# A streaming gradient kernel: the first store of every three tiles is issued after the second tile instead of the first

## The chip, the core and the metric

The kernel runs on one core of a Trainium2 chip. The metric is the device time of one execution in microseconds (us). The core's engines that do anything here are VectorE (DVE in the profile), GpSimd (POOL) and SyncE (SP), which only issues DMAs. All transfers between device memory and the on-chip memory go through the core's 16 DMA engines.

## What is computed

The input `x` is an 8192 x 8192 array of float32, and the output is its gradient along the rows:

```python
def reference(x):
    return np.gradient(x, axis=1)
```

Inside a row, an output element is half the difference of its two neighbours, `(x[j+1] - x[j-1]) / 2`. The first and the last element of a row are the plain differences `x[1] - x[0]` and `x[m-1] - x[m-2]`. The kernel reads 268 MB and writes 268 MB.

## The kernel before

The 8192 rows are cut into 32 tiles (`nsets`) of 256 rows; each of the 128 partitions holds two whole rows (`R = 2`), 16384 numbers or 64 KB, so a tile is 8 MiB. There are three buffers, `slots` (`NB = 3`), and a tile `i` uses slot `i % 3`. A slot is 64 numbers wider than the tile: the input is loaded at an offset of `SH = 64`, and the result is written in place at offset 0.

For each tile, in this order:

- `load(i)` (L60) brings the tile into its slot. It waits until the store of tile `i - 3`, which used the slot before, has landed.
- On POOL, `tensor_sub` (L70) takes the four plain differences of a partition's two rows and keeps them in the small buffer `ends`. It starts when the load has landed.
- On DVE, one custom instruction (L81) forms the halved differences of all 16382 inner elements of a partition. It follows the POOL instruction, since it overwrites the input.
- A copy (L92) puts the four numbers from `ends` into the result. The engine for it, `placer`, is POOL for tiles with `i % 5` of 1 or 3 (up to tile 29) and for tile 30, and DVE for the others.
- A store (L94) sends the tile out. It waits for the copy.

The last two tiles, 30 and 31, are done in two halves (one row of each partition at a time), each with its own copy and store of 4 MiB.

All loads and stores are issued by SP and go through one DMA queue, in program order: three loads, then, group by group, three stores and the three loads of the next group. The order is written out by hand (`tc.manual_schedule()`), and `chain` keeps only the waits that are needed. SP issues in order, so a store that waits holds up what stands behind it on SP. I call three tiles that share a turn of the slots a group: tiles 0 to 2, 3 to 5, and so on, ten full groups, then tiles 30 and 31.

Of the kernel before, what the change touches and what calls it, by code (L numbers as in the profile page):

```python
# [1 line left out]

# [4 lines left out]


@with_exitstack
def kernel(  # L10
    ctx: ExitStack,
    tc: tile.TileContext,
    x: bass.AP,
    out: bass.AP,
):

    nc = tc.nc
    P = nc.NUM_PARTITIONS
    n, m = x.shape
    R = 2
    NB = 3  # L30
    SH = 64
    W = R * m
    nsets = n // (P * R)
    f32 = x.dtype

    x_sets = x.rearrange("(s p t) m -> s p (t m)", p=P, t=R)
    out_sets = out.rearrange("(s p t) m -> s p (t m)", p=P, t=R)

    pool = ctx.enter_context(tc.tile_pool(name="pool", bufs=1))
    slots = [pool.tile([P, SH + W], f32, name=f"slot{k}", tag=f"slot{k}") for k in range(NB)]  # L40
    ends = pool.tile([P, nsets, R, 2], f32, name="ends", tag="ends")
    loads, stores = [], [None] * nsets
    in_front = {}

    def chain(i, ins, *needed):

        group, engine = f"slot{i % NB}", ins.ins.engine
        keep = [o.ins for o in needed]  # L50
        if in_front.get(engine, (None,))[0] == group:
            keep.append(in_front[engine][1])
        tc.declare_no_dep(ins.ins, group=group, keep=keep, reason="implied by the needed step")
        tc.add_to_no_dep_group(group, ins.ins)
        in_front[engine] = group, ins.ins
        return ins

    def load(i):
        b = slots[i % NB]
        ins = nc.sync.dma_start(out=b[:, SH : SH + W], in_=x_sets[i])  # L60
        loads.append(chain(i, ins, *([stores[i - NB]] if i >= NB else [])))

    with tc.manual_schedule():
        for i in range(NB):
            load(i)
        for i in range(nsets):
            b = slots[i % NB]
            xin = b[:, SH : SH + W].rearrange("p (t m) -> p t m", m=m)

            ins = nc.gpsimd.tensor_sub(  # L70
                out=ends[:, i, :, :],
                in0=xin[:, :, 1 : m : m - 2],
                in1=xin[:, :, 0 : m - 1 : m - 2],
            )
            at = [chain(i, ins, loads[i])]
            last = i >= nsets - 2
            nr = 1 if last else R
            for r in range(0, R, nr):
                c0, c1 = r * m + 1, (r + nr) * m - 1

                ins = nc.vector._custom_dve(  # L81
                    dve_ops.TENSOR_TENSOR_REDUCE_SUB_MAX,
                    out=b[:, c0:c1],
                    in0=b[:, SH + c0 + 1 : SH + c1 + 1],
                    in1=b[:, SH + c0 - 1 : SH + c1 - 1],
                    s0=0.0,
                    s1=0.5,
                )
                halved = chain(i, ins, *at)
                res = b[:, r * m : (r + nr) * m].rearrange("p (t m) -> p t m", m=m)  # L90
                placer = nc.gpsimd if i % 5 in (1, 3) and not last or i == nsets - 2 else nc.vector
                ins = placer.tensor_copy(out=res[:, :, 0 : m : m - 1], in_=ends[:, i, r : r + nr, :])  # L92
                placed = chain(i, ins, halved)
                ins = nc.sync.dma_start(  # L94
                    out=out_sets[i, :, r * m : (r + nr) * m], in_=b[:, r * m : (r + nr) * m]
                )
                stores[i] = chain(i, ins, placed)
                at = [halved]
            if i % NB == NB - 1:
                for k in range(i + 1, min(i + 1 + NB, nsets)):  # L100
                    load(k)


# [1 line left out]
_INS = ['x']  # L105
_OUTS = [((8192, 8192), 'float32')]


# [23 lines left out]
```

## Time and profile before

| what | value |
|---|---|
| time, median of 3 runs | 1247.57 us (1247.11 to 1249.06) |
| span of the profiled execution | 1245.5 us |
| DMA queue, share of 16 engines' span | 99.7%, 536.88 MB, 431 GB/s |
| DVE busy | 554.8 us, 45% |
| POOL busy | 17.7 us, 1% |
| a DVE instruction of a whole tile (L81) | 17.22 us, 30 times |
| a copy of the ends (L92), on DVE / on POOL | 0.17 / 0.19 us |

The span runs from the first to the last instruction of one profiled execution; the time of a run is some 2 us longer than it. The profile's timeline lists instructions with start, duration, engine, line, operation and tiles, and in brackets the idle time ahead of an instruction and what ended it. SPq is SyncE's queue; its rows merge several DMA issues into one ("x3"), so that the start is that of the first issue and the duration reaches to the last. A POOL row of L70 starts when a load has landed.

### The profile page before, as it was taken

How to read it: one execution, taken by the hardware profiler on the slowest of the kernel's cores; microseconds unless marked ns; L12 is line 12 of the kernel's file. 1: busy time of each engine (PE TensorE's matmuls, PEld its weight loads, DVE VectorE, ACT ScalarE, POOL GpSimd, SP SyncE). 2: the span in 40 equal slices, each digit the busy share in tenths (PEclk: the TensorE clock that was granted, in tenths of full speed). 3: DMA queues.
4: the chain of work that ended last, by engine and by line, in shares of the span. 5: the costliest groups of instructions: out<-in, count | busy, mean ns of one | idle time of the engine just before them, and what ended most of it. 6: DMA issues, size and time to landing. Idle time of an engine off the chain costs nothing.

```text
span 1245.5 us, 244 instructions
## 1 busy us (share of the span) xinstructions
DVE 554.8 (45%) x54; POOL 17.7 (1%) x50
## 2 busy tenths in 40 slices
DVE  2850583079009702850582079009603840591083
POOL 0000000000000000000000000000000000000020
DMA  9999999999999999999999999999999999999999
GB/s 404 438 436 434 413 436 438 438 438 436 434 427 434 425 438 438 436 438 438 427 425 434 431 438 438 438 436 429 427 431 431 438 436 436 436 429 434 434 396 404
DMA packets 9505, 536.88 MB, mean 431 GB/s; under 512 B 1056, under 2 KB 1056, under 8 KB 1056
## 3 DMA queue, kind: packets, MB, share of 16 engines
q1 hardware_dynamic: 9504, 536.88, 99.7%
q14 instruction: 1, 0.01, 0.0%
HBM read 268.44 MB, written 268.44 MB: 431 GB/s over the span
## 4 chain that ended last, share of the span: by engine, by line
another core or an unknown queue 74%; DVE 19%; DMA 3%; POOL 1%; issue 0%; SPq 0%; POOLq 0%
DVE slot L81 19%; DMA slot<-in_x_dram 3%; POOL slot L92 1%; POOL ends L70 0%; SPq L60 0%; DVE slot L92 0%; POOLq L127 0%
## 5 line engine op out<-in xcount | busy, mean ns | idle before, releaser
L81 DVE CUSTOM_DVE_ANT_0 slot<-slot 128x16382 f32<-128x16382 f32 (+1 forms) x34 | 551.5, 16219 | 668.4 <-POOL ends L70 668.3
L70 POOL TENSOR_TENSOR ends<-slot 128x4 f32<-128x4 f32 x32 | 6.3, 198 | 971.5 <-DMA slot<-in_x_dram 971.5
L92 POOL COPY slot<-ends 128x4 f32<-128x4 f32 (+1 forms) x14 | 11.2, 798 | 216.7 <-DVE slot L81 216.6
L92 DVE COPY slot<-ends 128x4 f32<-128x4 f32 (+1 forms) x20 | 3.4, 171 | 0.7
L116 POOL MEMSET const-float32-0.0<- 128x1 f32 x1 | 0.1, 99 | 0.2 <-issue 0.2
L116 POOL MEMSET const-bfloat16-1.0<- 128x1 bf16 x1 | 0.1, 102 | 0.0
L116 POOL MEMSET const-uint8-127<- 128x1 uint8 x1 | 0.1, 102 | 0.0
L116 POOL MEMSET const-float32-1.0<- 128x1 f32 x1 | 0.1, 98 | 0.0
## 6 DMA issues: line engine op xcount, KB each, us to landing
out_dram<-slot SPq DMA_DIRECT2D x4, 4096.0 KB, 20.2
slot<-in_x_dram SPq DMA_DIRECT2D x32, 58.0
out_dram<-slot SPq DMA_DIRECT2D x30, 40.4
```

Of the source, the lines that this page charges most:

```text
L70: ins = nc.gpsimd.tensor_sub(out=ends[:, i, :, :], in0=xin[:, :, 1 : m : m - 2], in1=xin[:, :, 0 : m - 1 : m - 2],)
L81: ins = nc.vector._custom_dve(dve_ops.TENSOR_TENSOR_REDUCE_SUB_MAX, out=b[:, c0:c1], in0=b[:, SH + c0 + 1 : SH + c1 + 1], in1=b[:, SH + c0 ...
L92: ins = placer.tensor_copy(out=res[:, :, 0 : m : m - 1], in_=ends[:, i, r : r + nr, :])
L116: nc = _bacc.Bacc("TRN2", target_bir_lowering=False, num_devices=1)
```

## The change

Stores move into a helper. For full groups, the store of the first tile is no longer issued when the first tile's copy is done, but with the second tile's: it waits for the first tile's copy and, by an added dependency, for the second tile's copy too. The second and third stores wait for their own copies as before, and the order on the queue and the transfers are the same. The rule for the engine of the copy changes as well: POOL copies the first tile of each group (`i % 3 == 0`, which takes in tile 30), DVE the other two. Tiles 30 and 31 keep their halves and their own stores.

```diff
+    def store(i, placed, cols=slice(0, W)):
+        ins = nc.sync.dma_start(out=out_sets[i, :, cols], in_=slots[i % NB][:, cols])
+        stores[i] = chain(i, ins, placed)
+        return ins
...
-                placer = nc.gpsimd if i % 5 in (1, 3) and not last or i == nsets - 2 else nc.vector
+                placer = nc.gpsimd if i % NB == 0 else nc.vector
                 ins = placer.tensor_copy(out=res[:, :, 0 : m : m - 1], in_=ends[:, i, r : r + nr, :])
                 placed = chain(i, ins, halved)
-                ins = nc.sync.dma_start(
-                    out=out_sets[i, :, r * m : (r + nr) * m], in_=b[:, r * m : (r + nr) * m]
-                )
-                stores[i] = chain(i, ins, placed)
                 at = [halved]
+                if last:
+                    store(i, placed, slice(r * m, (r + nr) * m))
+            if i % NB == 1 and not last:
+                opener = store(i - 1, first)
+                tc.add_manual_dep(
+                    opener.ins,
+                    placed.ins.name,
+                    mybir.DependencyInfo(mybir.DependencyClass.Sync, mybir.DependencyReason.DATA),
+                    reason="the first store of a group goes behind the second tile's difference",
+                )
+            first = placed
+            if i % NB and not last:
+                store(i, placed)
```

More of the change, by code (lines that the diff above doesn't have):

```diff
@@ L4 @@
 import concourse.tile as tile
-from concourse import bass_utils, dve_ops
+from concourse import bass_utils, dve_ops, mybir
 from concourse._compat import with_exitstack
@@ L90 @@
                 res = b[:, r * m : (r + nr) * m].rearrange("p (t m) -> p t m", m=m)
-                placer = nc.gpsimd if i % 5 in (1, 3) and not last or i == nsets - 2 else nc.vector
+                placer = nc.gpsimd if i % NB == 0 else nc.vector
                 ins = placer.tensor_copy(out=res[:, :, 0 : m : m - 1], in_=ends[:, i, r : r + nr, :])
                 placed = chain(i, ins, halved)
-                ins = nc.sync.dma_start(
-                    out=out_sets[i, :, r * m : (r + nr) * m], in_=b[:, r * m : (r + nr) * m]
-                )
-                stores[i] = chain(i, ins, placed)
-                at = [halved]
+                at = [halved]
+                if last:
[7 more added lines that the diff above has]
+                    reason="the first store of a group goes behind the second tile's difference",
+                )
+            first = placed
+            if i % NB and not last:
+                store(i, placed)
             if i % NB == NB - 1:
```

## The prediction

> **What bounds the kernel now.** I read the page first, then the timeline of one group of three tiles, then the end of the run. The page says that the DMA queue is the limit:
>
> ```profile
> span 1245.5 us, 244 instructions
> DVE 554.8 (45%) x54; POOL 17.7 (1%) x50
> q1 hardware_dynamic: 9504, 536.88, 99.7%
> ```
>
> The one hardware queue keeps the 16 DMA engines occupied for 99.7% of the span, while VectorE (DVE) works 45% of it. So no compute instruction matters by itself. What can matter is the few microseconds in which a DMA engine moves nothing, or moves slower than its pace.
>
> The timeline of tiles 3, 4 and 5 shows where those are. Columns: start, duration, engine, line, operation, tiles. The row of POOL L70 starts as soon as a load has landed, so I use it as the landing clock.
>
> ```profile
> 157.40 0.19 POOL L92 COPY slot<-ends 128x4 f32<-128x4 f32 x1 [17.32 <-DVE slot L81]
> 157.62 39.11 SPq L94 DMA_DIRECT2D out_dram<-slot  x3
> 159.24 0.20 POOL L70 TENSOR_TENSOR ends<-slot 128x4 f32<-128x4 f32 x1 [1.65 <-DMA slot<-in_x_dram]
> 159.47 17.22 DVE L81 CUSTOM_DVE_ANT_0 slot<-slot 128x16382 f32<-128x16382 f32 x1 [2.13 <-POOL ends L70]
> 176.72 0.17 DVE L92 COPY slot<-ends 128x4 f32<-128x4 f32 x1
> 178.71 0.20 POOL L70 TENSOR_TENSOR ends<-slot 128x4 f32<-128x4 f32 x1 [19.27 <-DMA slot<-in_x_dram]
> ```
>
> Load 4 has landed at 159.24, load 5 at 178.71. The store of tile 3 is issued at 157.62, so it sits in the queue behind load 5 for 21 us before it can move.
>
> Now the pace. Load 0 has landed at 22.62 and the last load, 31, at 1205.91; 61 transfers of 8 MiB lie between. Taking the landing rows of all second and third loads of a group, third minus second is 20.52 in the first group (62.46 - 41.94), and then 19.47, 19.58, 19.64, 19.94, 20.19, 19.56, 19.54, 19.33, 19.43. The five transfers from a third load to the next second load take 96.59 to 96.79 us (for example 275.42 - 178.71 = 96.71), which is 19.34 each. So the third load, and it alone, is stretched: by 1.18 us in the first group and by 0.13, 0.24, 0.30, 0.60, 0.85, 0.22, 0.20, -0.01 and 0.09 in the other nine, which add up to 2.62. Together 3.80 us. Check: 22.62 + 61 x 19.34 + 3.80 = 1206.2, and the row says 1205.91. All the time that this change can win back is in this 3.80 us.
>
> What is special about a third load? It is the only one that has a store queued behind it. The trace has a control for that, the last load:
>
> ```profile
> 1186.58 0.20 POOL L70 TENSOR_TENSOR ends<-slot 128x4 f32<-128x4 f32 x1 [77.07 <-DMA slot<-in_x_dram]
> 1195.56 8.91 POOL L92 COPY slot<-ends 128x2 f32<-128x2 f32 x2 [8.79 <-DVE slot L81]
> 1204.29 19.89 SPq L94 DMA_DIRECT2D out_dram<-slot  x4
> 1205.91 0.20 POOL L70 TENSOR_TENSOR ends<-slot 128x4 f32<-128x4 f32 x1 [1.44 <-DMA slot<-in_x_dram]
> ```
>
> Load 31 is also followed by a store, but that store is issued only at 1204.29, because the POOL copy that it waits for ran beside DVE and took 8.7 us. Load 31 took 1205.91 - 1186.58 = 19.33: no stretch. That is the order of events that the change makes everywhere.
>
> **What a late store costs.** Queued late, a store may find engines that have run dry. A table of short stretches prices the start; its last two columns count a packet where it begins, so a stretch with a rate is one in which packets start.
>
> ```profile
> 0.74:1.70 0.96, 0.00 (x0) 0.00 (x0) 1.00 0.00 0
> 1.70:2.40 0.70, 0.00 (x0) 0.00 (x0) 1.00 4.28 1498
> 1204.29:1205.10 0.81, 0.00 (x0) 0.18 (x1) 1.00 0.00 0
> 1205.10:1205.35 0.25, 0.00 (x0) 0.00 (x0) 1.00 4.63 1966
> 1205.35:1205.50 0.15, 0.00 (x0) 0.00 (x0) 1.00 0.51 218
> ```
>
> At the end of the run, 15 engines (1966 GB/s x 0.25 us = 15 packets of 32 KB) begin the store 0.8 to 1.06 us after its issue. The trace's rows of single packets put them at 0.85 to 0.99. The sixteenth begins at 1205.48, the moment it is done with load 31; that is 0.43 before the landing row. At the start of the run the same step takes longer: issue at 0.74, packets from 1.75 to 2.38, so 1.0 to 1.64.
>
> **The change, part by part.**
>
> *The first store of a group waits for the second tile's copy, ten times.* In the group shown, the new issue is at 176.72 + 0.17 + 0.03 = 176.92 instead of 157.62. By the end-of-run row its packets can begin at 177.77 to 177.91. Load 5 without the stretch has landed at 159.24 + 19.34 = 178.58, and its slowest engine is done 0.43 earlier, at 178.15. So the slowest engine, which sets the pace, has 0.24 us to spare; the faster ones wait up to half a microsecond, which costs nothing because they were ahead. Cost of the wait by this row: 0. By the start-up row: 176.92 + 1.64 = 178.56, that is 0.41 us late, and the first load had a slow first packet too (22.62 - 0.74 - 1.64 - 19.34 - 0.43 = 0.47). So 0.88 per hand-over, 8.8 us in ten. I take the end-of-run row, because it is this very hand-over, a store behind a load on running engines.
>
> [...]
>
> *The stretch goes.* In groups two to ten that is up to -2.62. Something may be left, since the store now arrives about 0.24 us before the slowest engine is done. I leave +0.2 for all nine. In the first group the 1.18 is four times the mean of the others, and it is the first write of the run; part of that may be a cold start that merely moves into the store. The cold first load paid 0.47 in its first packet, so I take -1.18 + 0.6 = -0.6, with ends 0 and -1.18.
>
> *The queue behind the waiting store.* SP's next instruction is the second store, which waits for the same DVE copy (176.89) in both kernels, so nothing is held up. It now issues some 0.4 us after the first one and isn't needed before the first has moved, 19 us later. The next load waits for the first store to land, near 198, and has two stores, 38 us, ahead of it in the queue.
>
> *The copies change engines.* POOL now copies the first tile of each group and tile 30, DVE all others: ten copies of 0.19 us on POOL instead of twelve, twenty of 0.17 on DVE instead of eighteen. DVE has about 2 us free between two tiles of a group (2.13 above) and 60 between groups; cost 0. The POOL copy at 157.40 falls in that 2 us. Were that cover gone, it would run beside DVE as at 1195.56, but the store waits for that DVE instruction anyway. Tiles 30 and 31 keep copies and stores as they are.
>
> Sum: -2.62 + 0.2 - 0.6 = -3.0 us on a span of 1245.5. The median of the runs is 1247.57, 2.1 above the span, and I carry this over: 1244.6 us.
>
> **The rivals.**
>
> *The stretch belongs to the change of direction, not to the early issue.* Then it stays wherever a load is followed by a store, and nothing is gained: 1247.6. For it: two groups show almost none, so it isn't tied rigidly to a queued store. Against it: load 31, 19.33 us. A partial stretch left behind, or a first group that keeps all its 1.18 together with half of the rest, falls here too: -1.3, 1246.3.
>
> *The engines run dry at each hand-over.* One mechanism, at the ten hand-overs: the store's packets begin later than load 5's slowest engine is done. Price by the start-up row 8.8, less the 3.8 of stretch that is gone: +5.0, 1252.6. It breaks even at 0.38 us per hand-over, when the last engine begins more than 1.6 us after the issue, and is measurably slower from 0.63 (2.5 us more in all). For it: the margin is a mere 0.24 us. Against it: the end-of-run row, 15 engines within 0.99 us.
>
> **How the numbers follow.** A measurement of this kernel can tell about 0.2% from no change, 2.5 us. The forecast, 0.68: between -2.5 and -3.8, so 1243.8 to 1245.1, faster by over 0.2%. The first rival 0.20, within 0.2%. The second 0.12, slower. The low end takes the whole 3.80 and 0.8 for the spread of medians (the runs before lie 1247.11 to 1249.06): 1243.0. The high end takes in the first rival and hand-overs of about 0.5 us late (10 x 0.5 - 3.8 = +1.2): 1248.8.
>
> **What would show it.** In the changed profile the third loads should take 19.3 to 19.4 us after the second ones, the first group's perhaps 19.9; the first stores should be issued 17.7 us after the second load's landing row; the distance from one third load to the next should be near 6 x 19.34 = 116.0 (before: 116.02 to 116.87). It would be wrong if that distance were above 116.4, with the following transfers landing late (the queue ran dry), or if third loads were as long as before (the direction, not the early issue).

## The result, and the profile after

The changed kernel took 1254.69 us (1254.36 to 1255.09) against 1248.74 us for the kernel before, five runs each (the 1247.57 above is the median of the first three): a ratio of 1.0051, 95% interval 1.0040 to 1.0061. It is slower by half a percent. The forecast was 1244.6 us, faster.

The page after, its head and the lines of VectorE and the DMA queue:

```profile
span 1252.8 us, 236 instructions
DVE 555.2 (44%) x56; POOL 17.4 (1%) x48
q1 hardware_dynamic: 9504, 536.88, 99.7%
```

The queue reads 99.7% again, although the span is 7.3 us longer. In the trace's rows the packets' times from start to end add up to 99.7% of 16 engines' span in both kernels, so a packet that takes too long (3122 ns instead of 2418 in the mean of the third stores' last ones, see below) looks as busy as one at full pace. This line can't show the loss.

The timeline of the same group, tiles 3 to 5 (L75, L86, L97 and L64 are the old L70, L81, L92 and L94):

```profile
157.89 0.19 POOL L97 COPY slot<-ends 128x4 f32<-128x4 f32 x1 [17.32 <-DVE slot L86]
159.73 0.20 POOL L75 TENSOR_TENSOR ends<-slot 128x4 f32<-128x4 f32 x1 [1.64 <-DMA slot<-in_x_dram]
177.22 0.17 DVE L97 COPY slot<-ends 128x4 f32<-128x4 f32 x1
177.46 19.64 SPq L64 DMA_DIRECT2D out_dram<-slot  x3
179.07 0.20 POOL L75 TENSOR_TENSOR ends<-slot 128x4 f32<-128x4 f32 x1 [19.14 <-DMA slot<-in_x_dram]
...
257.44 0.20 POOL L75 TENSOR_TENSOR ends<-slot 128x4 f32<-128x4 f32 x1 [78.17 <-DMA slot<-in_x_dram]
```

The hand-over that the prediction worked on went as forecast. The first store is issued at 177.46, 17.7 us after the second load's landing row. The third load takes 179.07 - 159.73 = 19.34 us: no stretch. All ten third loads now take 19.34 or 19.35, the first group's too, and their excess over 19.34 adds up to 0.08 us instead of 3.80.

The loss is in the next stretch of the same lines. From the third load's landing to the next group's first load lie four transfers: three stores and a load. They take 257.44 - 179.07 = 78.37 us. Before it was 256.07 - 178.71 = 77.36, which is four times 19.34; the first of these landings is this row of the kernel before:

```profile
256.07 0.20 POOL L70 TENSOR_TENSOR ends<-slot 128x4 f32<-128x4 f32 x1 [77.17 <-DMA slot<-in_x_dram]
```

Over the ten groups this excess is 10.63 us, and -0.33 us before. The sum closes: 10.63 + 0.33 - (3.80 - 0.08) = 7.24 us, and the span grew by 7.3.

Which of the four transfers is it? The tables of short stretches count packets where they begin, so each burst is the start of one round of 16 packets. These stretches hold the last two rounds of the third store and the first round of the load behind it, after and then before (last column GB/s):

```profile
231.40:231.90 0.50, 0.00 (x0) 0.00 (x0) 1.00 4.85 2097
231.90:233.90 2.00, 0.00 (x0) 0.00 (x0) 1.00 0.00 0
233.90:234.40 0.50, 0.00 (x0) 0.00 (x0) 1.00 6.21 2097
234.40:236.80 2.40, 0.00 (x0) 0.00 (x0) 1.00 0.00 0
236.80:237.70 0.90, 0.00 (x0) 0.00 (x0) 1.00 2.77 1165
```

```profile
230.40:231.50 1.10, 0.00 (x0) 0.00 (x0) 1.00 2.20 953
231.50:232.80 1.30, 0.00 (x0) 0.00 (x0) 1.00 0.00 0
232.80:233.90 1.10, 0.00 (x0) 0.00 (x0) 1.00 2.20 953
233.90:235.30 1.40, 0.00 (x0) 0.00 (x0) 1.00 0.00 0
235.30:236.30 1.00, 0.00 (x0) 0.00 (x0) 1.00 2.44 1049
```

By the trace's rows of single packets, the first packets of the bursts before begin at 230.57, 232.98 and 235.40: the pace of 2.42 us goes on across the change from store to load. After, they begin at 231.63, 234.05 and 236.96, and the last burst reaches to 237.66. The last packet of the third store is late by half a microsecond to a whole one (the step from 234.05 to 236.96 is 2.91, not 2.42).

Single packets make it exact. Chained end to start, the trace's packet rows fall on 16 engines. A packet of 64 KB takes 2418 ns. The mean excess over ten groups and 16 engines, in ns:

| packet | before | after |
|---|---|---|
| last of the third load | 254 | 1 |
| last of the first and the second store | 0, 0 | 4, 5 |
| last of the third store | 0 (97% at 0) | 704 (5% to 95%: 407 to 1089) |
| other packets of the three stores, on the average | 0 | 8 |
| first of the load behind the stores | 4 | 106 |

So before, something is paid at the change from load to store (254 ns), and after, at the change from store to load, 58 us later. The second price is higher (704 ns), and it is not idle time between the two: the next load, issued at 198.36, has been in the queue for 38 us, and the pause from the end of a store's packet to the start of the load's is 20 ns in the mean of the ten changes.

### The profile page after: what moved, and what is told of

It is laid out like the page before. It is cut to its first block, busy times and chain, and to the rows that moved or that the text cites. A ratio compares the mean times of both kernels' runs of the same rounds, so it can differ in the third digit from the quotient of the medians.

```text
span 1252.8 us, 236 instructions
## 1 busy us (share of the span) xinstructions
DVE 555.2 (44%) x56; POOL 17.4 (1%) x48
## 3 DMA queue, kind: packets, MB, share of 16 engines
q1 hardware_dynamic: 9504, 536.88, 99.7%
## 4 chain that ended last, share of the span: by engine, by line
another core or an unknown queue 79%; DVE 14%; DMA 3%; POOL 1%; issue 0%; SPq 0%; POOLq 0%
DVE slot L86 14%; DMA slot<-in_x_dram 3%; POOL slot L97 1%; POOL ends L75 0%; SPq L60 0%; DVE slot L97 0%; POOLq L141 0%
## 5 line engine op out<-in xcount | busy, mean ns | idle before, releaser
L86 DVE CUSTOM_DVE_ANT_0 slot<-slot 128x16382 f32<-128x16382 f32 (+1 forms) x34 | 551.5, 16220 | 675.2 <-POOL ends L75 675.2
L75 POOL TENSOR_TENSOR ends<-slot 128x4 f32<-128x4 f32 x32 | 6.4, 200 | 1013.8 <-DMA slot<-in_x_dram 1013.8
L97 POOL COPY slot<-ends 128x4 f32<-128x4 f32 (+1 forms) x12 | 10.8, 901 | 182.0 <-DVE slot L86 182.0
L97 DVE COPY slot<-ends 128x4 f32<-128x4 f32 (+1 forms) x22 | 3.8, 172 | 0.8
```

Of the source, the lines that this page charges most:

```text
L75: ins = nc.gpsimd.tensor_sub(out=ends[:, i, :, :], in0=xin[:, :, 1 : m : m - 2], in1=xin[:, :, 0 : m - 1 : m - 2],)
L86: ins = nc.vector._custom_dve(dve_ops.TENSOR_TENSOR_REDUCE_SUB_MAX, out=b[:, c0:c1], in0=b[:, SH + c0 + 1 : SH + c1 + 1], in1=b[:, SH + c0 ...
```

## Experiments

Theories, as the expectations call them. 1: the late issue is the cause. 2: the new placing of copies is. A: the first store must be queued well before the engines are done with the load ahead of it. Of A there are two forms. A1: engines that wait at the hand-over are lined up in time and pay for that. A2: an engine has a lead only while its next transfer is queued early enough; one that gets the store too late loses it, also when it doesn't wait, and pays for that when the next load begins. The expectations call this lead a read-ahead, of reads over writes; that is my guess, and no row here shows the two apart.

**The two parts of the change alone.**

```diff
 before.py, copies only:
-  placer = nc.gpsimd if i % 5 in (1, 3) and not last or i == nsets - 2 else nc.vector
+  placer = nc.gpsimd if i % NB == 0 else nc.vector
 after.py, wait only: the same edit backwards
```

> The kernel before with only the new rule for the engine of the copy (POOL for the first tile of each group, DVE for the others); the stores are issued as before. Theory 1, the late issue of the first store is the cause: no change, 1248 us, last packets of third stores not stretched. Theory 2, the copies are the cause: 1254.7 us as in the changed kernel.

> The changed kernel with the old rule for the engine of the copy, so that only the late issue is left. Theory 1 (late issue): 1254 to 1255 us, the last packet of each third store stretched by 0.4 to 1.1 us. Theory 2 (copies): 1248 us.

Copies only: ratio to before 0.9997 (0.9988 to 1.0006). Wait only: 1254.90 us, 1.0056 (1.0039 to 1.0073); third stores' last packets 713 ns too long on the average. Theory 1 holds; the copies cost nothing.

**The time of issue, in steps.** The second tile's DVE instruction is cut in two, and the first store waits for the first part only.

```diff
+  cuts = [c0, CUT, c1] if i % NB == 1 and not last else [c0, c1]
+  for d0, d1 in zip(cuts, cuts[1:]):
       (the same instruction on columns d0:d1)
+      if d1 == CUT:
+          opener = store(i - 1, first)   # waits for this part
```

> The second tile's difference is cut into two DVE instructions of 8191 columns, and the first store waits only for the first of them: issued about 8.6 us earlier than in the changed kernel, 10 us later than before. Theory A, what counts is that the store is in the queue well before the engines have read the last of the load ahead of it: as before, 1247 to 1249 us, third loads stretched, third stores not. Theory B, what counts is that first and second store are issued one right after the other or that the first waits for DVE: still 1254 us.

> The same cut at column 13100: the first store is issued about 3.5 us earlier than in the changed kernel, about 5 us before the slowest engine is done with the third load. Theory A2: all engines are past the threshold, so as before, 1246.5 to 1249 us, third loads stretched, third stores not. If the loss falls off slowly with the lead: some stretch of the third stores is left and the time is 1249 to 1250 us.

> As the half-way kernel, but the cut is at column 14746 of 16382, so the first store is issued about 1.7 us earlier than in the changed kernel; its packets could begin 1 to 2 us before the load ahead is done, so no engine runs dry. Theory A1, engines that wait at the hand-over are lined up, and lined-up engines pay at the end of the stores: no wait, so no stretch of the third stores, 1245 to 1248 us. Theory A2, the read side must run ahead into the store before the load's last data have come, some 1 to 2 us before its end: partly or wholly as the changed kernel, 1250 to 1255 us, third stores stretched though no engine waits.

> As the nine-tenths kernel with the cut at column 15400: the first store is issued about 1.0 us earlier than in the changed kernel, about 2.6 us before the slowest engine is done with the third load. From the rows of single packets of the runs so far: an engine that gets the store 2.1 to 2.7 us before its own end loses about 0.1 us per group in all, one that gets it 3 us before or earlier loses 0.15 to 0.3 at the end of the load, one that gets it 1.2 us before or later loses 0.6 to 0.9 at the end of the stores. Theory A2 (the read side must run ahead, at a threshold near 2 us): 1245 to 1247.5 us, the best so far. Theory A1 (engines that wait are lined up and pay): the same or better. If lateness alone costs in proportion, between the changed kernel and the nine-tenths kernel: 1251 to 1253 us.

> The same cut at column 15890: the first store is issued about 0.5 us earlier than in the changed kernel, about 2.0 us before the slowest engine is done and 1.4 before the fastest; its packets begin about 1 us after the issue, so no engine should wait. Theory A1 (only engines that wait pay): 1245 us. Theory A2 (read side): slowest engine loses 0.15 to 0.3 us per group at the end of the third store, the others 0.6, so 1246 to 1250 us with third stores stretched and no gaps.

The columns of excess are sums over ten groups of one profiled execution, from the landing rows, as above. "Ahead" is the mean time from the first store's issue to the third load's landing row. The ratios go by the medians of several runs, each against runs of the kernel before taken beside them, and a profiled execution can lie off its median: at 14746 it was the fastest of ten (1249.04 us, median 1250.47), at 15400 it took 1250.80 (median 1248.81).

| CUT | ahead, us | third loads, excess us | stores and next load, excess us | ratio to before |
|---|---|---|---|---|
| none, first tile (before) | 21.4 | 3.80 | -0.33 | 1 |
| 8192 | 10.8 | 4.23 | -0.57 | 0.9997 (0.9988 to 1.0007) |
| 13100 | 5.7 | 4.07 | -0.46 | 0.9999 (0.9990 to 1.0008) |
| 14746 | 4.0 | 4.05 | 0.40 | 1.0017 (1.0007 to 1.0026) |
| 15400 | 3.2 | 3.59 | 2.86 | 1.0007 (0.9998 to 1.0016) |
| 15890 | 2.4 | 0.37 | 5.91 | 1.0014 (1.0005 to 1.0024) |
| none, second tile (after) | 1.6 | 0.08 | 10.63 | 1.0051 (1.0040 to 1.0061) |

The two prices trade places within 4 us. Five microseconds ahead is as good as twenty. My hope for the cut at 15400, 1245 to 1247.5 us, failed: it took 1248.81. The engines reach the end of the third load up to 2.4 us apart in that profile, so one time of issue can't suit all of them, and the fast ones pay at the stores.

The packets of the three last cuts sort the engines by the time from the issue to each engine's own end of the third load (groups two to ten, means in ns):

| issue ahead of own end, us | engines | wait | last packet of load | last packet of third store |
|---|---|---|---|---|
| under 0.9 | 95 | 298 | 0 | 730 |
| 0.9 to 1.2 | 20 | 5 | 0 | 642 |
| 1.2 to 1.5 | 63 | 6 | 0 | 507 |
| 1.5 to 1.8 | 124 | 6 | 1 | 347 |
| 1.8 to 2.1 | 59 | 6 | 1 | 177 |
| 2.1 to 3.0 | 52 | 6 | 40 | 72 |
| 3.0 to 3.6 | 15 | 6 | 337 | 0 |
| over 3.6 | 4 | 6 | 1088 | 18 |

This decides against A1: engines that got the store 1.2 to 1.8 us early didn't wait (6 ns in the mean; in the kernel before, a step from transfer to transfer takes about 2), and still paid 0.35 to 0.5 us at the end of the stores. Nor do they pay for the waits of others: in six of the ten groups of the 15890 profile no engine waited at all, and the last packets of their third stores are 255 to 557 ns too long in the mean. Being lined up doesn't decide either. In the first group at 13100 the 16 engines begin the last packet of the third store within 0.52 us and lose nothing; in the third group at 15400 they are spread over 2.32 us and lose 526 ns. It is the time of queueing that counts, with a soft threshold near 2 us: the price at the stores falls from 507 ns at 1.2 to 1.5 us to 72 at 2.1 to 3.0.

The two prices together are least between 2.1 and 3.0 us ahead, 0.11 us. In the first group at 14746 all engines got the store 2.6 to 3.5 us ahead, and by the landing rows that group lost 0.36 us in all, against 1.24 in the kernel before.

**Run dry elsewhere.** If A2 is right, the loss doesn't need the hand-over from load to store. Here that hand-over is as early as before, and the third store is held back until the second has landed.

```diff
 before.py
+  if i % NB == NB - 1 and not last:
+      tc.add_manual_dep(ins.ins, stores[i - 1].ins.name, ...)
```

> The kernel before, but the third store of each full group is issued only when the second has landed, so the engines run dry between these two stores, inside the store phase; the hand-over from loads to stores is as early as before. The dry stretch itself costs about 1.5 to 2 us in each of ten groups, so about 1265 us. Theory A2 (an engine that starts a store from nothing has lost its read-ahead, and pays when the next load begins): last packets of third stores stretched by 0.4 to 1.1 us, as in the changed kernel, and the third stores' packets a few ns longer, though the hand-over from load to store was early. If the loss is tied to the hand-over from load to store alone: third stores' last packets not stretched.

It took 1279.75 us in a single run, more than expected. The landing rows of tiles 13, 14 and 15:

```profile
520.48 0.20 POOL L70 TENSOR_TENSOR ends<-slot 128x4 f32<-128x4 f32 x1 [19.16 <-DMA slot<-in_x_dram]
540.65 0.20 POOL L70 TENSOR_TENSOR ends<-slot 128x4 f32<-128x4 f32 x1 [2.46 <-DMA slot<-in_x_dram]
620.53 0.20 POOL L70 TENSOR_TENSOR ends<-slot 128x4 f32<-128x4 f32 x1 [79.69 <-DMA slot<-in_x_dram]
```

The four transfers take 79.88 us, 2.52 more than 77.36; by the packets 1.64 of it is the dry stretch in this group. The last packet of the third store is 737 ns too long on the average of all groups, as in the changed kernel. So the loss follows the dry queue inside the store phase too, as A2 expects. What I had not priced: the third load is stretched as well, 540.65 - 520.48 = 20.17, 10.23 us over ten groups. Before, it was 1.18 in the first group and 0.29 in the mean of the others. Here every group pays the price of a first group.

**One late group.** This suggests that the lead is a state, won once and kept while the queue doesn't run dry.

```diff
 after.py
-  if i % NB == 1 and not last:      (late first store)
+  if i == 13:
-  if i % NB and not last:           (store at once)
+  if i != 12 and not last:
```

> The changed kernel with the late issue in one group only, tiles 12 to 14; in the other groups the first store is issued as soon as its copy is done. Theory, the engines' read-ahead is a state that is won once at a hand-over from load to store at the price of about 1.1 us, is kept through loads and stores while the queue does not run dry, and is lost in the late group: the third load of the late group is not stretched (19.35 us), the four transfers from it to the next first load take about 1 us more than 77.36, and the third load of the group after it pays the price of a first group again, 0.8 to 1.2 us, more than the others' mean of 0.3. If nothing is kept from group to group: the group after the late one has a stretch like the others. The time is 1248 to 1251 us in both.

1251.37 us in a single run. Landing rows of the late group (tiles 12 to 14) and the one behind it, from its timeline of POOL:

```profile
508.83 0.20 POOL L75 TENSOR_TENSOR ends<-slot 128x4 f32<-128x4 f32 x1 [1.63 <-DMA slot<-in_x_dram]
528.18 0.20 POOL L75 TENSOR_TENSOR ends<-slot 128x4 f32<-128x4 f32 x1 [19.15 <-DMA slot<-in_x_dram]
606.66 0.20 POOL L75 TENSOR_TENSOR ends<-slot 128x4 f32<-128x4 f32 x1 [78.28 <-DMA slot<-in_x_dram]
...
626.02 0.20 POOL L75 TENSOR_TENSOR ends<-slot 128x4 f32<-128x4 f32 x1 [1.64 <-DMA slot<-in_x_dram]
646.57 0.20 POOL L75 TENSOR_TENSOR ends<-slot 128x4 f32<-128x4 f32 x1 [20.35 <-DMA slot<-in_x_dram]
724.01 0.20 POOL L75 TENSOR_TENSOR ends<-slot 128x4 f32<-128x4 f32 x1 [77.24 <-DMA slot<-in_x_dram]
```

Late group: 19.35 for the third load, then 78.48, 1.12 too long. Next group: 20.55 for the third load, 1.21 too long, then 77.44. One late hand-over costs twice, once at its own next load and once to win back what was lost. In the packets of the next group all engines pay, 1126 ns on the average; in the other groups behind the first it is 108 to 443. (By the landing rows alone the ninth group comes close, with 1.03 us; there only the slowest engines pay, 217 ns on the average.) This is one late group in one execution; in the run with the late third store, every group shows the same pair of prices.

**A piece of the store early.** Part of the first store is issued at once, the rest late; `load` waits for both.

```diff
 after.py
+  if i % NB == 0 and not last:
+      store(i, placed, slice(0, 2048))        # 4096, 8192 in the others
-  opener = store(i - 1, first)
+  opener = store(i - 1, first, slice(2048, W))
```

> The changed kernel, but the first 2048 of the 16384 columns of a group's first tile are stored as soon as that tile's copy is done (as in the kernel before); the rest of this store waits for the second tile's copy as in the changed kernel. The small piece keeps the DMA engines busy for 2.4 us behind the third load, so the rest is queued some 3.5 us before they could run dry. Read-ahead theory: third stores not stretched, third loads stretched, about as the kernel before: 1247 to 1249.5 us. If issuing seven eighths of the store late is what costs: 1254 us.

> As the small-piece kernel with 4096 columns stored early. If the size of the early packets (8 KB per row in the small-piece kernel, 16 KB here, 32 KB in the half-piece kernel) decides what is kept, the stretch of third loads in groups two to ten lies between those of the two other kernels; if nothing but chance decides, it is anywhere from 0.3 to 1 us and unrelated to the size.

> As the small-piece kernel, but half of the first tile's columns (8192 of 16384) are stored early, so 9.7 us of transfer are queued behind each third load, and the other half is issued late. The small-piece kernel's profiled execution had third loads stretched by about 1 us in every group, and third stores not. If the read-ahead is kept from group to group whenever the queue never runs dry: third loads stretched by 1.1 us in the first group and 0.3 in the mean of the others, 1248 us. If cutting the store in two makes every hand-over pay like a first one: 1 us in every group, 1254 us.

| columns early | time, us | third loads, excess us | stores and next load, excess us |
|---|---|---|---|
| 2048 | 1250.38 (1247.67 to 1254.34), ratio 1.0012 (1.0002 to 1.0022) | 9.75 | 0.25 |
| 4096 | 1249.93 (one run) | 4.96 | 0.68 |
| 8192 | 1249.00, ratio 1.0004 (0.9994 to 1.0014) | 4.49 | 0.66 |

With 2.4 us of transfer (an eighth of 19.34) queued early, the stores' loss is gone by the landing rows (0.25 against 10.63 us). That is the point of the experiment: seven eighths of the store may be issued late if something is there to bridge the gap. The packets show how much bridge it takes, and the threshold of 2 us a second time, at another place in the queue. No engine of the 2048 profile waited for the rest of the store (9 ns at most). Yet where the rest was issued less than 1.5 us before an engine was done with its small piece, the last packet of the third store is 711 ns too long in the mean (23 engines); from 1.5 to 2.0 us it is 229 (64), from 2.0 to 2.5 us 31 (22), and beyond 2.5 us 0 (51). The slowest engine has the longest time ahead, so the landing rows don't show this.

The time, 1250.38 us, was above the 1247 to 1249.5 that I expected: the profiled execution of the smallest piece paid about 1 us at every third load, though its engines did not run dry. It was the slowest of the kernel's ten runs, so its rows aren't typical of the median. With larger pieces only the first group and a few others pay so much. That engines which came under 2 us lost their lead would explain later groups, but the second group paid 1.01 us behind a first one without a loss. Why it did is not settled.

No version beat the kernel before by more than the interval.

## Why the prediction was wrong

*What bounds the kernel* was right: 3.80 us of stretch in third loads was all that could be won, and it needs a store queued early behind them. With the store late, the stretch vanished in all ten groups, as the control with load 31 had said. The first rival, that the stretch belongs to the change of direction, is refuted by the 0.08 us that are left.

*The cost of the wait, taken as 0 from the end-of-run row*, was right for the hand-over itself. A table of short stretches of the changed kernel shows the start of the first store, issued at 177.46:

```profile
177.46:178.25 0.79, 0.00 (x0) 0.00 (x0) 1.00 0.01 0
178.25:178.65 0.40, 0.00 (x0) 0.00 (x0) 1.00 6.18 2621
```

All 16 packets (2621 GB/s x 0.40 us is 16 x 64 KB) begin 0.79 to 1.19 us after the issue, and the last one, at 178.61, follows its engine's load without a pause. The 15 others begin by 178.45, so the slowest engine had 0.16 us to spare; 0.24 had been predicted.

*The sum failed because it had no term for the end of the store phase.* The step that failed is "The queue behind the waiting store": it asked whether SP's later instructions are held up, found that they have 38 us to spare, and took the transfers behind to be unchanged. They were not. The missing term is about 1.1 us per group, 10.96 us in ten (10.63 + 0.33), against the 3.72 that were won. The sum had no such term, and gave no reason why the load behind the stores should stay as it was.

*The control misled for the same reason.* Behind load 31 come only stores. No load follows a late store in the kernel before, so the trace could not show what a late store does to the next load. The row priced half of the event.

*The second rival*, the engines run dry at each hand-over, had the right sign and was nearest in size (1252.6), but named the wrong place. It looked for the price at the hand-over, in late starts and a slow first packet. The first store's first packet is about 0.05 us too long, not 0.47; the price appears where the stores end, and engines that never ran dry pay it too. The prediction's sign for this rival, a distance above 116.4 us from one third load to the next, did show (296.14 - 179.07 = 117.07), but for another reason than a queue that ran dry.

*The first group.* I took half of its 1.18 us for a cold start that would move into the store. The stretch went entirely: the first third load took 19.35 us. About the size of my term did turn up, but not in the store. The four transfers behind that load take 1.68 us too long, 0.69 more than the mean of the other groups (0.99), and by the packets the extra is in the first packet of the load behind the stores: 307 ns too long in the mean, 678 at most, against 83 in the mean of the later groups. The run with the late issue alone has it too (1.78 against 1.00). Its cause is not settled, so the size was luck. That the price at the third load needs no cold start is shown by the experiment with one late group, where it comes back, 1.21 us, in the middle of the run.

What is shown and what is argued: shown are the place of the loss (704 ns in the last packet of the third store), its threshold near 2 us, that it needs no idle engine, and that it follows a dry queue inside the store phase as well; that a late hand-over makes the next one dear is shown by two profiles. That the thing lost is a lead of reads over writes inside each DMA engine is not shown, and stays a guess. Two numbers fit it. With the late issue, a step from store to store costs 4 to 5 ns in the last packet of one store and 13 to 33 ns in the first of the next, and only the step to a load costs 0.7 us. And the first load of all, which has no transfer ahead of it, has a first packet that is 0.58 us (before) or 0.63 us (after) too long, about the same size.

## What to carry to other kernels

On a queue that is the bound (99.7% here), a transfer that is issued "just in time" may still cost where it starts without a gap (here the slowest engine had 0.16 us to spare, and a group lost about 1.1 us): look for the loss at the next change of direction, not only at the hand-over, and by packet or landing times, since the busy share didn't move here. Keep a transfer queued some microseconds ahead; in this kernel 5 us was as good as 20, and 2 us was the edge, counted to the end of each DMA engine's own work and not to the landing of the whole transfer. And when a row of the trace serves as a control, check that what follows the event in it is the same, not only what leads up to it.

## What was not expected of the hardware

The third store's last packet takes 0.7 us longer when the first of the three stores was queued less than about 2 us before the engines were done with the load ahead, 58 us earlier (704 ns in the mean of the changed kernel), and the stores' other packets take 2426 ns on the average instead of 2418. An early store has its own price at the end of the load ahead, by the landing rows: 1.18 us in the first group of the kernel before, 1.21 us in the group behind the one late group, 1.02 us in the mean of the ten groups of the kernel with the late third store, and 0.29 us in the mean of later groups of the kernel before.
